# Attention's entry of a hybrid S5 and attention layer: keys in turn with the first queries, values last, y's copies issued later

## The chip, the cores and the metric

The kernel runs on one core of a Trainium2 chip. The metric is the device time of one execution in microseconds (us). The kernel before was timed three times: 1645.6, 1643.4 and 1640.19 us, median 1643.4 us.

## The reference

The layer takes two sequences of 512 tokens (one "prompt", one "sample", treated alike) with model width 1024 and computes, in float32:

```python
h = rms_norm(x, ln1)
q, k, v, u, g_att, g_ssm = jnp.split(h @ w_in, IN_SPLITS, axis=-1)
q = rms_norm(q.reshape(bsz, seq_len, N_HEADS, HEAD_DIM), q_gain)       # 16 heads of 64
k = rms_norm(k.reshape(bsz, seq_len, N_KV_HEADS, HEAD_DIM), k_gain)    # 4 key-value heads
y_att = windowed_attention(q, k, v, sink, bias, mask)   # blocks of 128 queries, 3 blocks of keys
y_ssm = s5_branch(u, ...)                               # scan both ways, gelu, then GLU with w_glu
mixed = sigmoid(g_att) * y_att + sigmoid(g_ssm) * y_ssm
x = x + mixed @ w_out
h2 = rms_norm(x, ln2)
return x + square(relu(h2 @ w_up)) @ w_down
```

The windowed attention adds a relative bias to the scores, takes a softmax with a sink logit for each head and multiplies with the values. A query head's norm runs over its own 64 columns.

## The kernel before

All 1024 tokens are handled together. A float32 product is made from three matmuls of rounded parts: every operand is split into a high part (a copy that rounds it, ACT) and a low part (the rest, a subtraction on DVE), and high x high, high x low and low x high are summed in PSUM. So each weight that is loaded costs, besides its DMA into a raw tile (`w_raw`, or `c_raw` for a 128-column block; both in the tag `c_raw`, two buffers), a cast on ACT and a subtraction on DVE.

The program runs in this order: the norm, the gates and u; the S5 branch, whose result y goes to DRAM (`y_scr`); attention, with the S5 branch's GLU entering at its end; w_out; the MLP. The change is at the seam between the S5 branch and attention, lines 499 to 762.

**Attention's entry before.** The keys' weights are loaded (`load_qkv`, L519) into the pool `cpool`, tags `c_hi` and `c_lo`, two halves of 4 x 128 rows each; then eight key tiles K0 to K7 of 128 tokens are projected (`proj_qkv`, 24 matmuls of 128x256 each, lines 164 to 166) into a PSUM slot `acc` (three of them) and normed (`head_rms`, L503: square on ACT, sum on DVE L509, add and power on POOL L511 and L512, product on DVE L514 into `kn`). The values follow in the same manner, with weights in the pool `ap`, tiles V0 to V7, copied out by ACT (L551) and DVE (L552). Then come the eight copies that reorder y in DRAM (`y2_scr` from `y_scr`, L744 and L745, 512 KB each, issued from SP), the query weights of the first key-value head (`weight_pieces(0)`, four pieces of 256 rows, into `cpool`), four bias tables (L582), and the turned keys (`key_copies` on POOL L588, `key_turn`: four transposes on PE L597, a copy on ACT L598, a subtraction on DVE L599).

Last in the entry, four query tiles Q0 to Q3 of the first step are made one after the other (L752 to L762). A tile (class `Tile`) is projected (24 matmuls, L615), squared (ACT L621), summed (DVE L625), raised to a power (POOL L627, L628), multiplied (DVE L632), doubled by a copy (POOL L633) and turned (four transposes on PE into a slot `acc`, L638), then copied out by ACT (L643) and DVE (L647). For Q0 to Q2 the turn stands right behind the tile's own norm; Q3's turn is left for the first step.

**The steps.** There are eight steps, one for each key-value head and sequence, and four units of 128 queries in each. PE, ACT and DVE follow an order written out by hand (L778 on): a unit's scores (L668), maximum (DVE L672), exponentials (ACT L678), while PE also turns the previous unit's weights and multiplies with its values and projects a query tile of the next step between them. SP and POOL follow an order that the scheduler chooses. One piece of a later step's query weights is loaded in each unit (`pieces_of`); in all of this `weight_pieces(j)` uses `cpool` for even heads j and `ap` for odd ones. In the second unit of a step the previous step's sums are inverted and sent through DRAM (`rs_scr` L729, `fac` L734), and POOL multiplies the step's output by them (L739, 128x1024 elements) and SP writes it (`mix_scr`, L740).

**The end of attention.** The reordered y is loaded in eight pieces (`yr`, L889) and cast (ACT L894, DVE L895), and the GLU begins (L901 on): its weight columns go through `cpool`'s `c_hi` and `c_lo` (L137 to L139), and its inputs `mx` are loaded from DRAM (L909).

## Time and profile before

| | us |
|---|---|
| median of three runs | 1643.4 |
| the profiled execution, its own time | 1645.35 |
| its span (first to last instruction) | 1643.5 |
| PE busy in the span | 1524.7 |
| DVE busy | 1145.3 |
| ACT busy | 796.1 |
| POOL busy | 172.8 |

The profiled execution's mean granted TensorE clock is 0.975 of full speed. In a row of the timeline the first two numbers are the start and the duration in us, counted from the start of the span; the bracket gives the idle time of the engine just before and what ended it. In the list of waits, the three numbers are the total, the count and the longest. In a table of windows, each engine has its busy time and, in brackets, its number of instructions, and PEclk is the share of full speed that the clock gate granted.

In the trace, the first key tile of the entry's uninterrupted part (K3) starts at 479.69 us, the keys' turn follows the last value tile at 518.51 us, the first query tile starts at 520.39 us, and the second unit of the first step starts its scores at 560.10 us.

### The profile page before, as it was taken

Reading aid. Unit: us, or ns where it says so; the run is one execution under the profiler, and the core shown is the slowest. Engines: PE = TensorE matmul, PEld = TensorE weight load, DVE = VectorE, ACT = ScalarE, POOL = GpSimd, SP = SyncE. Lnnn points to the kernel's source line nnn. Section 1 sums busy time; section 2 is a strip of 40 time slices with the busy share of each in tenths; the row PEclk is TensorE's granted clock in tenths of the full one; section 3 lists DMA queues with packets and bytes.
Section 4 is the critical chain, followed back from the end, with each engine's and each line's share of the span. In section 5 each row is a group of like instructions: output and inputs, shape, how many; then the busy total and the mean of one; then the engine's idle time right before and its main releaser. Section 6 shows DMA issues by size and latency. Waiting matters only on the chain.

```text
span 1643.5 us, 22428 instructions
## 1 busy us (share of the span) xinstructions
PE 1524.7 (93%) x8202; PEld 1295.5 (79%) x8202; DVE 1145.3 (70%) x2006; ACT 796.1 (48%) x1398; POOL 172.8 (11%) x246
## 2 busy tenths in 40 slices
PE   4999999999778799998788998999999999999999
PEld 3778878888777798896565898788888888888787
DVE  7899969952432488989787564877777759666644
ACT  5667752222322488878555322555445544433332
POOL 2000001000021233332354000000000000000000
PEclk9999999999889899999889999999999999999999
DMA  4444457224772021223556322355444397445331
GB/s 156 130 149 150 143 176 270 90 103 133 270 248 88 14 71 46 92 66 103 199 192 221 132 91 103 116 159 162 160 142 146 118 353 273 154 133 187 118 126 64
DMA packets 115226, 240.24 MB, mean 146 GB/s; under 512 B 15355, under 2 KB 38011, under 8 KB 115116
## 3 DMA queue, kind: packets, MB, share of 16 engines
q1 hardware_dynamic: 93100, 191.47, 36.3%
q10 hardware_dynamic: 19456, 37.87, 6.1%
q0 software_dynamic: 2560, 9.48, 1.7%
q8 instruction: 64, 1.05, 0.2%
q14 instruction: 46, 0.38, 0.1%
HBM read 169.53 MB, written 81.82 MB: 153 GB/s over the span
## 4 chain that ended last, share of the span: by engine, by line
PE 72%; DVE 9%; DMA 6%; issue 6%; ACT 4%; POOL 2%; SPq 0%; ACTq 0%; POOLq 0%; DVEq 0%
PE bank L165 12%; PE bank L164 12%; PE bank L166 12%; PE acc L164 7%; PE acc L165 7%; PE acc L166 7%; PE acc L615 4%; DMA ctab_in<-ct_scr 2%; PE sps L389 2%; PE sps L409 2%; PE po L700 2%; PE sps L487 2%; PE sps L668 1%; PE tps L684 1%; PE acc L638 1%
## 5 line engine op out<-in xcount | busy, mean ns | idle before, releaser
L165 PE MATMUL bank<-b_lo,a_hi 128*128 128x512 f32 x448 | 174.7, 390 | 1.4 <-DVE b_lo L1118 1.4
L166 PE MATMUL bank<-b_hi,a_lo 128*128 128x512 f32 x448 | 174.3, 389 | 0.0
L164 PE MATMUL bank<-b_hi,a_hi 128*128 128x512 f32 x448 | 173.5, 389 | 0.0
L165 PE MATMUL acc<-hT,c_hi 128*128 128x512 f32 x384 | 152.1, 396 | 0.0
L164 PE MATMUL acc<-hT,c_hi 128*128 128x512 f32 x384 | 151.9, 396 | 0.0
L166 PE MATMUL acc<-hT,c_lo 128*128 128x512 f32 x384 | 150.2, 391 | 0.4 <-DVE c_lo L139 0.4
L164 PE MATMUL bank<-act,u_hi 128*128 128x512 f32 x376 | 147.2, 392 | 2.6 <-ACT u_hi L1015 2.6
L165 PE MATMUL bank<-act,u_hi 128*128 128x512 f32 x376 | 146.9, 391 | 0.0
L1117 ACT CAST a_hi<-d_a 128x1024 fp32r<-128x1024 f32 x56 | 59.2, 1057 | 181.1 <-PE bank L165 177.9
L166 PE MATMUL bank<-act,u_lo 128*128 128x512 f32 x376 | 146.6, 390 | 0.0
L1118 DVE TENSOR_TENSOR a_lo<-d_a,a_hi 128x1024 fp32r<-128x1024 f32 x56 | 68.5, 1224 | 99.2 <-ACT a_hi L1117 99.2
L615 PE MATMUL acc<-w_hi,hT 128*128 128x256 f32 x512 | 121.2, 305 | 3.6 <-ACT w_hi L573 3.6
L165 PEld LDWEIGHTS bank<-b_lo,a_hi 128*128 128x128 f32 x448 | 84.1, 188 | 19.9 <-DVE b_lo L1118 2.6
L164 PEld LDWEIGHTS bank<-b_hi,a_hi 128*128 128x128 f32 x448 | 84.1, 188 | 17.6
L166 PEld LDWEIGHTS bank<-b_hi,a_lo 128*128 128x128 f32 x448 | 84.1, 188 | 17.4
L615 PEld LDWEIGHTS acc<-w_hi,hT 128*128 128x128 f32 x512 | 91.1, 199 | 7.8 <-ACT w_hi L573 4.0
L139 DVE TENSOR_TENSOR c_lo<-c_raw,c_hi 128x512 fp32r<-128x512 f32 x80 | 62.5, 785 | 46.0 <-ACT c_hi L138 45.7
L138 ACT CAST c_hi<-c_raw 128x512 fp32r<-128x512 f32 x80 | 49.2, 620 | 81.0 <-PE acc L165 56.1
L164 PEld LDWEIGHTS bank<-act,u_hi 128*128 128x128 f32 x376 | 71.0, 189 | 18.0 <-ACT u_hi L1015 3.2
L164 PEld LDWEIGHTS acc<-hT,c_hi 128*128 128x128 f32 x384 | 72.3, 188 | 15.6 <-issue 1.5
L166 PEld LDWEIGHTS acc<-hT,c_lo 128*128 128x128 f32 x384 | 72.1, 188 | 15.3 <-DVE c_lo L139 0.7
L165 PEld LDWEIGHTS acc<-hT,c_hi 128*128 128x128 f32 x384 | 72.3, 188 | 15.1 <-issue 1.1
(292 smaller groups left out, 3909.5 us busy)
## 6 DMA issues: line engine op xcount, KB each, us to landing
d_a<-a_scr SPq DMA_DIRECT2D x56, 512.0 KB
u_raw<-in_w_up_dram SPq DMA_DIRECT2D x32, 512.0 KB
a_scr<-t ACTq DMA_DIRECT2D x64, 256.0 KB
k<-in_w_down_dram SPq DMA_DIRECT2D x32, 512.0 KB
c_raw<-in_w_ug_dram SPq DMA_DIRECT2D x48, 256.0 KB
a_scr<-a ACTq DMA_DIRECT2D x48, 256.0 KB
ct_scr<-ctab SPq DMA_DIRECT2D x16, 576.0 KB
ctab_in<-ct_scr SPq DMA_DIRECT2D x16, 576.0 KB
```

The costliest lines, as they stand in the source:

```text
L138: S.copy(hi[:, sl, :], raw)
L139: sub(lo[:, sl, :], raw, hi[:, sl, :].bitcast(F32))
L164: PE.matmul(ps, a[0], b[0], start=first, stop=False)
L165: PE.matmul(ps, a[0], b[1], start=False, stop=False)
L166: PE.matmul(ps, a[1], b[0], start=False, stop=last)
L389: PE.matmul(ps[0:48, g * 144:(g + 1) * 144], lbt[:, ri, q * SG + gp * SH + g, :], ctab[:, gp * SH + g, ri].rearrange("p n c -> p (n c)"), ...
L409: PE.matmul(ps[:, i * P:(i + 1) * P], bm[:, ri, g, :], u_sb[:, gp * SH + g, :], start=True, stop=True)
L487: PE.matmul(o, ctab[:, g0 % SI + g, ri, 0:T * CH], st[:, ri, g].rearrange("p s k -> p (s k)"), start=False, stop=ri == 1)
L615: PE.matmul(self.ps, hT[sq][act][:, k, col:col + P], w[:, k % 4, :], start=i == 0, stop=i == 3 * KT - 1)
L700: PE.matmul(self.po, vv, self.hl[i][part], start=i + part == 0, stop=i == self.nkb - 1 and part == 1)
L1117: S.copy(hi, src)
L1118: V.tensor_sub(lo, src, hi.bitcast(F32))
```

## The change

The entry is written in another order. The four key tiles of the first sequence come first; then each query tile Q0 to Q3 is followed by one of the key tiles K4 to K7, and a query tile is turned only after the next query tile's projection. The keys are turned after K4. The values' weights and V0 to V7 come last. The values' weights now go half into the two buffers of the tag `ev` and half into `cpool`; the query weights of even heads go into `ap` and of odd heads into `cpool`, the other way round than before. y's eight copies are written one to a unit in the second and third steps (i = 1 and 2).

```diff
-        def load_qkv(src, even):
+        def load_qkv(src, homes):
             halves = []
             for e in range(2):
-                pool = cpool if even else ap
-                hi = pool.tile([P, KT // 2, CB], F32R, tag="c_hi", name="w_hi")
-                lo = pool.tile([P, KT // 2, CB], F32R, tag="c_lo", name="w_lo")
+                pool, tags = homes[e]
+                hi, lo = [pool.tile([P, KT // 2, CB], F32R, tag=tag, name=name) for tag, name in zip(tags, ("w_hi", "w_lo"))]
...
-        def rows_blocks(blk, fn):
-            w = load_qkv(w_qkv[blk], blk == K_BLK)
-            for t in range(NT):
-                ps = acc()
-                proj_qkv(ps[:, 0:CB], w, hT[t // 4], (t % 4) * P)
-                fn(t, ps[:, 0:CB])
-
-        rows_blocks(K_BLK, lambda t, ps: head_rms(ps, kn[:, t]))
+        def rows_block(w, t, fn):
+            ps = acc()
+            proj_qkv(ps[:, 0:CB], w, hT[t // 4], (t % 4) * P)
+            fn(t, ps[:, 0:CB])
+
+        def k_evac(t, ps):
+            head_rms(ps, kn[:, t])
...
-        rows_blocks(V_BLK, v_evac)
...
-            pool = cpool if j % 2 == 0 else ap
+            pool = ap if j % 2 == 0 else cpool
...
-        for t in range(T):
-            SP.dma_start(y2_scr[:, :, t, :].rearrange("g c k -> c g k"), y_scr[t])
-
+        column = cpool, ("c_hi", "c_lo")
+        w_k = load_qkv(w_qkv[K_BLK], [column, column])
+        for t in range(4):
+            rows_block(w_k, t, k_evac)
         for piece in weight_pieces(0):
             piece()()
         load_biases(0)
-        key_turn(0, 0, key_copies(0, 0))
+        kd = key_copies(0, 0)
         rows = None
         for t in range(4):
             new = Tile(0, 0, t)
             new.project(3 * KT)
             new.square()
             new.power()
             new.norm()
-            if t < 3:
-                new.turn()
-                new.high()
-                new.low()
-        rows = new
+            if rows:
+                rows.turn()
+                rows.high()
+                rows.low()
+            rows = new
+            rows_block(w_k, 4 + t, k_evac)
+            if t == 0:
+                key_turn(0, 0, kd)
+        w_v = load_qkv(w_qkv[V_BLK], [(evp, ("ev", "ev")), column])
+        for t in range(NT):
+            rows_block(w_v, t, v_evac)
...
                 for qb in range(NB):
+                    if 1 <= i < 3:
+
+                        t = (i - 1) * NB + qb
+                        SP.dma_start(y2_scr[:, :, t, :].rearrange("g c k -> c g k"), y_scr[t])
```

Three places show what this makes of the engines' order. The first is PE at the turn of query tile Q0. Before, the transposes (L638) stand between the last matmuls of Q0 (`acc_4649`) and the first of Q1 (`acc_4691`):

```order
L615 MATMUL acc_4649<-w_lo_4620,hT0_0_109 128x256
L615 MATMUL acc_4649<-w_hi_4619,hT0_1_110 128x256
L638 MATMUL acc_4684<-ident_89,qn_4681 128x128 x4
L615 MATMUL acc_4691<-w_hi_4609,hT0_0_109 128x256
L615 MATMUL acc_4691<-w_lo_4610,hT0_0_109 128x256
```

In the changed kernel the same transposes (now L634, `qn_4295` is Q0's) stand behind all of K4, the turn of the keys and all of Q1 (`acc_4341`), and K5 (`acc_4383`, lines 164 to 166) follows:

```order
L611 MATMUL acc_4341<-w_lo_4244,hT0_0_109 128x256
L611 MATMUL acc_4341<-w_hi_4243,hT0_1_110 128x256
L634 MATMUL acc_4376<-ident_89,qn_4295 128x128 x4
L164 MATMUL acc_4383<-w_hi_4081,hT1_0_111 128x256
L165 MATMUL acc_4383<-w_lo_4082,hT1_0_111 128x256
L166 MATMUL acc_4383<-w_hi_4081,hT1_1_112 128x256
```

PE's whole sequence was K3 to K7, V0 to V7, the keys' turn, Q0, its turn, Q1, two scores of the first unit, Q1's turn, Q2, its turn, Q3; it is now K3, Q0, K4, the keys' turn, Q1, Q0's turn, K5, Q2, Q1's turn, K6, Q3, Q2's turn, K7, V0 to V7, and then the first unit.

The second place is SP, which issues the loads, around the first step's division (`row` into `rs_scr`, then `fac`, then `mix_scr`). Before, with all of y's copies issued long ago:

```order
L572 DMA w_raw<-in_w_qkv_dram 128x512 x7
L729 DMA rs_scr<-row 16x128
L734 DMA fac<-rs_scr 64x2x512 x2
L572 DMA w_raw<-in_w_qkv_dram 128x512
L740 DMA mix_scr<-ya 128x2x512
L582 DMA bias<-line_scr 128x384 x4
```

In the changed kernel (y's copies are L791, and a row prints both y buffers as `y_scr`):

```order
L791 DMA y_scr<-y_scr 16x64x128
L725 DMA rs_scr<-row 16x128
L568 DMA w_raw<-in_w_qkv_dram 128x512 x2
L791 DMA y_scr<-y_scr 16x64x128
L730 DMA fac<-rs_scr 64x2x512 x2
L578 DMA bias<-line_scr 128x384 x4
L736 DMA mix_scr<-ya 128x2x512
```

The load of `fac` now stands behind two loads of query weights and the last copy of y. The copies do not stand one to a unit as they are written: the scheduler has put the first ahead of the values' weights, the second and third between and behind these, and the others between the loads of the first and second steps' query weights.

The third place is POOL, at the same division's product. Before, it stands in the third unit of the second step, ahead of a tile's sum (`ms_5526`), and the turned keys' copy `kd_5674` of the third step comes eight instructions later:

```order
L660 COPY p_5635<-nsink_103 128x4
L739 TENSOR_TENSOR ya_4813<-ya_4813,fac_5389 128x1024
L627 TENSOR_SCALAR ms_5526<-ms_5526 128x4
L628 TENSOR_TENSOR rq_5528<-ms_5526,neg_half_94 128x4
L633 COPY qn_5558<-qn_5558 128x4x64
L660 COPY p_5744<-nsink_103 128x4
L627 TENSOR_SCALAR ms_5639<-ms_5639 128x4
L628 TENSOR_TENSOR rq_5641<-ms_5639,neg_half_94 128x4
L660 COPY p_5852<-nsink_103 128x4
L588 COPY kd_5674<-kn_4079 128x512
L633 COPY qn_5671<-qn_5671 128x4x64
```

In the changed kernel it stands right ahead of that copy, in the first unit of the third step:

```order
L656 COPY p_5742<-nsink_103 128x4
L623 TENSOR_SCALAR ms_5636<-ms_5636 128x4
L624 TENSOR_TENSOR rq_5638<-ms_5636,neg_half_94 128x4
L656 COPY p_5851<-nsink_103 128x4
L735 TENSOR_TENSOR ya_4805<-ya_4805,fac_5383 128x1024
L584 COPY kd_5671<-kn_4079 128x512
L629 COPY qn_5668<-qn_5668 128x4x64
```

From the next division on, POOL's order is that of before. One more thing moves far from the entry: since `cpool` now holds the odd heads' query weights, the casts of the GLU's first two weight columns (L138 on ACT, L139 on DVE, four of each) leave the fifth and sixth steps, where they stood among the units; they now stand in the last unit of the seventh step, in the eighth step, and, for the second column's subtractions, behind nearly all of the casts of `yr`.

## The prediction

> **What bounds the kernel now.** I read the page's totals first, and in the chain of work that ended last the shares by engine:

> ```profile
> PE 1524.7 (93%) x8202; PEld 1295.5 (79%) x8202; DVE 1145.3 (70%) x2006; ACT 796.1 (48%) x1398; POOL 172.8 (11%) x246
> PE 72%; DVE 9%; DMA 6%; issue 6%; ACT 4%; POOL 2%; SPq 0%; ACTq 0%; POOLq 0%; DVEq 0%
> ```

> PE bounds the whole, so the question is where PE stands still or runs slowly near the change. Next come the waits between 470 and 590 us, the rows with PE as the waiting engine:

> ```profile
> PE acc L638 <- POOL qn L633: 11.3, 5, 3.3
> ...
> PE acc L164 <- DVE kn L514: 4.2, 1, 4.2
> ...
> PE acc L615 <- ACT w_hi L573: 3.6, 2, 2.3
> ...
> PE acc L615 <- DVE w_lo L574: 1.0, 3, 0.5
> ```

> The 4.2 us is the wait ahead of K3, which stands at the same place in both orders. The other three rows are the four query tiles: 4.6 us for their weights, and 11.3 us for the normed tile ahead of each turn. Then the table of windows: the keys and values, the first query tile, the rest of the query tiles with the first unit, the second unit up to the next step, the steps after that, and the last step with the GLU's start.

> ```profile
> core 0: us, PE busy (x) PEld busy (x) DVE busy (x) ACT busy (x) POOL busy (x), PEclk, DMA share, GB/s
> 479.70:518.90 39.20, 39.20 (x316) 39.17 (x316) 10.44 (x24) 6.14 (x16) 10.39 (x15) 0.96 0.54 155
> 518.90:528.40 9.50, 4.86 (x26) 3.66 (x24) 3.76 (x6) 3.14 (x6) 0.00 (x0) 0.93 0.34 109
> 528.40:557.70 29.30, 18.21 (x105) 17.49 (x104) 7.34 (x19) 6.60 (x14) 7.17 (x13) 0.73 0.02 8
> 557.70:588.60 30.90, 30.36 (x225) 28.16 (x226) 26.40 (x66) 24.65 (x61) 7.91 (x17) 1.00 0.10 32
> 588.60:740.00 151.40, 147.89 (x1090) 136.25 (x1089) 133.74 (x348) 122.30 (x306) 53.48 (x94) 1.00 0.23 72
> 740.00:814.80 74.80, 63.98 (x325) 50.61 (x324) 58.77 (x120) 56.44 (x112) 20.10 (x23) 0.93 0.43 139
> ```

> In the third row PE is busy for 18.21 of 29.30 us, and at a clock of 0.73. So the query tiles lose twice: by waiting, and by running slowly after it. The timeline of PE shows how:

> ```profile
> 531.80 1.12 PE L638 MATMUL acc<-ident,qn 128*128 128x128 f32 x4 [3.28 <-POOL qn L633]
> ...
> 534.42 0.63 PE L615 MATMUL acc<-w_hi,hT 128*128 128x256 f32 x2
> 534.85 0.41 PE L615 MATMUL acc<-w_lo,hT 128*128 128x256 f32 x1
> ...
> 541.32 1.12 PE L638 MATMUL acc<-ident,qn 128*128 128x128 f32 x4 [3.11 <-POOL qn L633]
> ...
> 545.43 0.40 PE L615 MATMUL acc<-w_hi,hT 128*128 128x256 f32 x2
> 545.67 0.28 PE L615 MATMUL acc<-w_lo,hT 128*128 128x256 f32 x1
> 545.79 0.28 PE L615 MATMUL acc<-w_hi,hT 128*128 128x256 f32 x1
> 549.41 0.66 PE L638 MATMUL acc<-ident,qn 128*128 128x128 f32 x4 [3.35 <-POOL qn L633]
> ...
> 557.74 0.66 PE L638 MATMUL acc<-ident,qn 128*128 128x128 f32 x4 [1.39 <-POOL qn L633]
> 558.23 0.60 PE L597 MATMUL tps<-ident,kd 128*128 128x128 f32 x4
> 558.59 0.36 PE L615 MATMUL acc<-w_hi,hT 128*128 128x256 f32 x1
> ...
> 560.10 0.34 PE L668 MATMUL sps<-kh,qa 128*128 128x384 f32 x1
> ```

> Two matmuls take 0.43 us (534.42 to 534.85) after the first idle stretch, and 0.24 us (545.43 to 545.67) at full speed. The four waits for `qn` are 3.28 + 3.11 + 3.35 + 1.39 = 11.13 us; the 11.3 has one short wait more. With 4.6 us for the weights, PE waits 15.7 us in the entry.

> **The change part by part.** (1) **The entry.** I count PE's work from K3's start at 479.7 us to the second unit's scores at 560.1 us, 80.4 us. It is 5 key, 8 value and 4 query tiles and one tile of the next step: 18 x 24 = 432 matmuls of 0.12 us, 51.8 us; six turns of 0.36 us (558.23 to 558.59), 2.2 us; eight matmuls of scores, 1.0 us. Together 55.0 us. The rest, 80.4 - 55.0 = 25.4 us, is 15.7 us of waits and 9.7 us of half clock. Of the half clock some stays: the stretch up to 518.9 us has 13 tiles, 312 x 0.12 = 37.4 us, and the keys' turn, yet lasts 39.2 us. Its surplus, 39.2 - 37.4 - 0.4 = 1.4 us, follows the unchanged wait ahead of K3. So 25.4 - 1.4 = 24.0 us can go.

> Does it go? The turn of a query tile needs this chain, here for the third tile, whose last matmul starts at 545.79:

> ```profile
> 546.16 0.39 ACT L621 ACTIVATE sq<-acc 128x256 f32<-128x256 f32 x1 [3.00 <-PE acc L615]
> ...
> 547.40 1.04 POOL L628 TENSOR_TENSOR rq<-ms,neg_half 128x4 f32<-128x4 f32 x1
> 548.47 0.42 DVE L632 TENSOR_TENSOR qn<-acc,rq 128x256 f32<-128x256 f32 x1 [1.47 <-POOL rq L628]
> 548.96 0.40 POOL L633 COPY qn<-qn 128x256 f32<-128x256 f32 x1 [0.52 <-DVE qn L632]
> ```

> The turn starts 3.62 us after that matmul. Now two tiles stand between, 2 x 24 x 0.12 = 5.8 us: covered with 2 us to spare. The tighter chain is that of the three slots `acc`. A tile's slot is free when DVE's product ends, 548.89, some 3.0 us after PE could go on (545.91); in the new order one tile and one turn stand between the end of a slot's use and the next, 2.88 + 0.36 = 3.24 us. That leaves 0.2 us, and DVE also does the values' and queries' low parts there (about 0.7 us each, in its idle time mostly). Likewise the second half of the values' weights can be cast only after K7 has read its own, and PE has 30 matmuls of V0 to V2 (3.6 us) to do meanwhile. If all is hidden this costs nothing; if each of the eight slots in the alternation came 0.3 us late, 2.4 us. I take 0.6, near the hidden end, since the margin is positive. The query weights' 4.6 us goes: their loads stand ahead of y's copies in SP's order now. Before, they stood behind all of them:

> ```profile
> 481.02 11.44 SPq L745 DMA_DIRECT2D y_scr<-y_scr  x7
> 494.44 2.60 SPq L572 DMA_DIRECT2D w_raw<-in_w_qkv_dram  x2
> ```

> [...]

> (2) **The first unit's exponentials.** Before, they ran between the stalled query tiles:

> ```profile
> 537.69 0.28 PE L668 MATMUL sps<-kl,qa 128*128 128x256 f32 x1
> ...
> 538.58 1.28 ACT L678 ACT_TABLE_LOAD   x1 [0.43 <-DVE nmx L672]
> 539.88 0.51 ACT L678 ACTIVATE p<-p,nmx 128x257 f32<-128x257 f32 x1
> ...
> 558.87 0.69 ACT L598 ACTIVATE kh<-tps,gain_k 128x512 fp32r<-128x512 f32 x1 [2.31 <-PE tps L597]
> ```

> That cover is gone. ACT's table load starts 0.9 us after the scores, when the first maximum is there (538.58 - 537.69). Then ACT needs 1.28 us for it, 4 x 0.6 for the exponentials with their sums, and for the turned keys and Q3, which stand between them, 2 x 0.69: 6.0 us after the first scores. Meanwhile PE has 8 x 0.12 + 24 x 0.12 + 2 x 0.36 = 4.6 us of the first unit and 0.7 us of the second's scores (560.10 on, four of 128x384) before it turns the weights. So 0.7 us late, and a little more by the backlog on ACT and DVE: I take 1.0, between 0 and 2.

> (3) **POOL.** The division's product moves ahead of the third step's `kd` and `qn`:

> ```profile
> 602.52 2.41 POOL L739 TENSOR_TENSOR ya<-ya,fac 128x1024 f32<-128x1024 f32 x1 [0.40 <-DMA fac<-rs_scr]
> ...
> 614.05 0.61 POOL L588 COPY kd<-kn 128x512 f32<-128x512 f32 x1
> 614.61 0.40 POOL L633 COPY qn<-qn 128x256 f32<-128x256 f32 x1
> ```

> PE turns that tile at 615.06, when the copy of 614.61 has just ended, so it will stand 2.4 us; behind it wait the turn of the keys and all of PE's order. PE is busy 147.89 of 151.40 us there, so nothing gives it back. `fac` itself is issued later, behind two loads of weights and a copy of y, but has some 10 us until POOL gets there. I take 2.3, between 0 and 2.4.

> (4) **The GLU's first two columns.** Four casts (ACT) and four subtractions (DVE) leave a stretch where PE is nearly full and come into the last 75 us, where PE has 64 us of work, ACT 56 and DVE 59, and the chain goes back and forth. One of each:

> ```profile
> 695.42 0.62 ACT L138 CAST c_hi<-c_raw 128x512 fp32r<-128x512 f32 x1
> 807.00 0.69 DVE L139 TENSOR_TENSOR c_lo<-c_raw,c_hi 128x512 fp32r<-128x512 f32 x1 [2.01 <-ACT c_hi L138]
> ```

> 4 x 0.69 = 2.8 us is the most if DVE is the one that waits there; nothing if they fit its gaps. The third column's loads come later by their two buffers, too, about 1 us. I take 1.5, between 0 and 3.8.

> (5) **y's copies and the weights' homes** cost nothing by themselves: the copies are asynchronous, the DMA's share in the steps they move to is 0.02 to 0.23, and y is not read before the last steps.

> **The sum:** 24.0 - 0.6 - 1.0 - 2.3 - 1.5 = 18.6 us. The profiled execution (1645.35 us, of which 1643.5 is the span) would go to 1626.8; it stands 2 us above the median of the runs, so the median goes from 1643.4 to 1624.8, say 1625.

> **The rivals.** (a) All the covers hold: the product on POOL and the GLU's casts are hidden, and only part (2) costs. Gain 22 to 24 us, 1619 to 1621. For it speaks that the engines beside PE have idle time; against it that PE's turn at 615.06 had no slack at all.

> (b) The alternation doesn't run free: the slots `acc` come late by up to a microsecond at each of the eight tiles between K3 and V0, since ACT, DVE and POOL each take key and query tiles in strict order. Another 4 to 8 us, 1629 to 1633.

> (c) The clock doesn't come back. PE would wait a little at every tile, too short to matter by itself, but often. The matmuls from K3's end to the second unit, about 52 us, would take 52/0.73 = 71 us at the clock of the third row of windows: 19 us lost, 1644, no change. From a clock of about 0.64 on (81 us, 29 lost) it ends slower, and at 0.5 it is 1625 + 52 = 1677. Against it: in the steps after 588.6, PE has many short waits (3.5 of 151 us) at a clock of 1.00. [...]

> (d) The copies of y aren't spread as the change says: three of eight stand on SP among the entry's weights, and one each before the division's transfers. If these hold up the values' weights by a copy's share of the 11.44 us (1.6 us) each, that is 2 to 5 us more, 1627 to 1630.

> **How the numbers follow.** The forecast, with its own range of 1621 to 1628, has 0.58; (a) 0.14; (b) 0.11 and (d) 0.09; (c) 0.04 for no change and 0.04 for slower. About 0.3% (5 us) is what a measurement of this kernel can tell from no change. So faster is 0.92, same 0.04, slower 0.04. The range takes in (a) with the scatter of the runs below, and (b) above: 1617 to 1633.

> **What would show it.** In the changed profile: no wait of PE above 0.5 us between K3 and V7; a clock of 1.00 from about 483 us on; the second unit's scores at about 537 us instead of 560; a wait of PE for POOL's `kd` or `qn` of about 2.3 us some 55 us after that; and PE's wait at the GLU's start about as long as now. Waits for `kn` or `qn` at every tile would mean (b), a clock under 0.9 there (c), a wait for the values' weights (d).

## The result, and the profile after

The changed kernel takes 1624.5 us (median of four runs, 1619.4 to 1630.8) where the kernel before takes 1644.5 us in the same comparison (four runs). The ratio is 0.988 with an interval of 0.983 to 0.992. A second comparison on another occasion gave 1619.9 against 1643.0 us, ratio 0.985 (0.982 to 0.988). The prediction was 1625 us, faster.

The page of the changed kernel begins with the same picture as before, PE in front:

```profile
PE 1522.8 (93%) x8202; PEld 1293.8 (79%) x8202; DVE 1140.7 (70%) x2006; ACT 794.0 (49%) x1398; POOL 172.7 (11%) x246
```

Busy times hardly move (PE 1522.8 us after 1524.7): a PE that waits isn't counted as busy, so a wait that goes doesn't show in them. The span is only 14.5 us shorter than in the profile before, so it must be cut into pieces first. I cut at three events of PE: the start of K3, the first scores of the first step's second unit, and PE's restart after its long wait in the GLU. Here are those rows of the changed kernel's timeline, with the turns between them:

```profile
484.34 0.58 PE L164 MATMUL acc<-w_hi,hT 128*128 128x256 f32 x1 [4.18 <-DVE kn L514]
495.30 0.60 PE L593 MATMUL tps<-ident,kd 128*128 128x128 f32 x4
498.60 0.60 PE L634 MATMUL acc<-ident,qn 128*128 128x128 f32 x4
504.79 0.60 PE L634 MATMUL acc<-ident,qn 128*128 128x128 f32 x4
511.30 0.60 PE L634 MATMUL acc<-ident,qn 128*128 128x128 f32 x4
...
542.74 0.34 PE L664 MATMUL sps<-kh,qa 128*128 128x384 f32 x1
...
811.47 0.79 PE L164 MATMUL acc<-act,c_hi 128*128 128x512 f32 x1 [11.47 <-ACT c_hi L138]
```

No turn has a bracket any more: PE waits for no query tile in the entry. Before, K3 started at 479.69, the second unit at 560.10 and the GLU's restart was at 827.08. So the pieces are:

| us | before | after | difference |
|---|---|---|---|
| start to K3 | 479.7 | 484.3 | +4.7 |
| stage 1: K3 to the second unit's scores | 80.4 | 58.4 | -22.0 |
| stage 2: from there to the GLU's restart | 267.0 | 268.7 | +1.8 |
| the rest | 816.4 | 817.5 | +1.1 |
| span | 1643.5 | 1629.0 | -14.5 |

The first piece and the last wander: over all profiles shown below K3 starts between 475.0 and 484.3 us, whichever kernel it is, and the rest takes 814 to 821 us. Stage 1 and stage 2 are what the change touches. The waits of PE between 470 and 570 us are down to two rows:

```profile
PE acc L164 <- DVE kn L514: 4.2, 1, 4.2
...
PE sps L664 <- DVE nmx L668: 0.5, 1, 0.5
```

The first is the unchanged wait ahead of K3. The windows of the changed kernel, cut at the corresponding places (columns as before), show the clock:

```profile
484.30:523.50 39.20, 39.07 (x303) 38.60 (x304) 17.39 (x35) 10.62 (x22) 18.05 (x28) 0.93 0.35 101
523.50:536.00 12.50, 12.50 (x107) 12.50 (x106) 1.94 (x5) 1.86 (x5) 0.00 (x0) 1.00 0.29 88
```

PE is full from K3 on, and slow only at the start (0.93): the clock of 0.73 that stood over the query tiles is gone. The one new wait in the steps is that for POOL's product, in the timelines of POOL and PE:

```profile
596.97 2.37 POOL L735 TENSOR_TENSOR ya<-ya,fac 128x1024 f32<-128x1024 f32 x1
599.29 0.60 POOL L584 COPY kd<-kn 128x512 f32<-128x512 f32 x1
599.84 0.40 POOL L629 COPY qn<-qn 128x256 f32<-128x256 f32 x1
...
600.29 0.66 PE L634 MATMUL acc<-ident,qn 128*128 128x128 f32 x4 [2.19 <-POOL qn L629]
```

The product has no bracket: it waits for no load of `fac` and stands late by POOL's order alone. It ends, the two copies follow at once, and PE's turn starts when the second is done, after 2.19 us of standing still.

### The profile page after: what moved, and what is told of

It reads as the page before. It is cut to its first block, busy times and chain, and to the rows that moved or that the text cites. A ratio compares the mean times of both kernels' runs of the same rounds, so it can differ in the third digit from the quotient of the medians.

```text
span 1629.0 us, 22424 instructions
## 1 busy us (share of the span) xinstructions
PE 1522.8 (93%) x8202; PEld 1293.8 (79%) x8202; DVE 1140.7 (70%) x2006; ACT 794.0 (49%) x1398; POOL 172.7 (11%) x246
## 4 chain that ended last, share of the span: by engine, by line
PE 72%; DVE 8%; DMA 7%; issue 6%; ACT 4%; POOL 2%; SPq 0%; ACTq 0%; POOLq 0%; DVEq 0%
PE bank L165 12%; PE bank L166 12%; PE bank L164 12%; PE acc L165 7%; PE acc L166 7%; PE acc L164 7%; PE acc L611 4%; DMA ctab_in<-ct_scr 3%; PE sps L389 2%; PE sps L409 2%; PE sps L487 2%; PE po L696 1%; DMA k<-in_w_down_dram 1%; PE sps L664 1%; PE tps L680 1%
## 5 line engine op out<-in xcount | busy, mean ns | idle before, releaser
L164 PE MATMUL bank<-b_hi,a_hi 128*128 128x512 f32 x448 | 174.2, 391 | 0.0
L164 PE MATMUL acc<-hT,c_hi 128*128 128x512 f32 x384 | 152.6, 397 | 0.0
L164 PE MATMUL bank<-act,u_hi 128*128 128x512 f32 x376 | 147.6, 393 | 3.3 <-ACT u_hi L1022 3.3
L611 PE MATMUL acc<-w_hi,hT 128*128 128x256 f32 x512 | 116.1, 295 | 0.0
L164 PEld LDWEIGHTS bank<-b_hi,a_hi 128*128 128x128 f32 x448 | 84.5, 189 | 17.5
L139 DVE TENSOR_TENSOR c_lo<-c_raw,c_hi 128x512 fp32r<-128x512 f32 x80 | 60.9, 765 | 43.1 <-ACT c_hi L138 42.9
L611 PEld LDWEIGHTS acc<-w_hi,hT 128*128 128x128 f32 x512 | 87.0, 189 | 3.8
L138 ACT CAST c_hi<-c_raw 128x512 fp32r<-128x512 f32 x80 | 49.1, 618 | 83.5 <-PE acc L165 47.5
L164 PEld LDWEIGHTS bank<-act,u_hi 128*128 128x128 f32 x376 | 71.2, 189 | 18.7 <-ACT u_hi L1022 3.7
L164 PEld LDWEIGHTS acc<-hT,c_hi 128*128 128x128 f32 x384 | 72.7, 189 | 15.6 <-issue 1.5
```

What stands on the lines that cost most here:

```text
L138: S.copy(hi[:, sl, :], raw)
L139: sub(lo[:, sl, :], raw, hi[:, sl, :].bitcast(F32))
L164: PE.matmul(ps, a[0], b[0], start=first, stop=False)
L611: PE.matmul(self.ps, hT[sq][act][:, k, col:col + P], w[:, k % 4, :], start=i == 0, stop=i == 3 * KT - 1)
```

## The experiments

**The changed kernel once more.** No edit; it shows how far stages can be trusted.

> The changed kernel once more, to see how far the stages of two profiles agree. Stage 1 is the time from K3's first matmul to the first scores of the first step's second unit, stage 2 from there to PE's restart after its long wait in the GLU (11 to 12 us). In the two profiles so far stage 1 is 80.4 us before and 58.4 after, stage 2 is 267.0 before and 268.7 after. All theories: 58.4 +- 1 and 268.7 +- 1, whatever comes ahead of K3 (which started 4.7 us later in the profile after). If the stages themselves wander by several us, the sum of the prediction met the median by chance.

Measured: stage 1 58.35 us, stage 2 270.98 us. K3 started at 477.21 us, 7 us earlier than in the first profile, and stage 1 is the same to 0.1 us. Stage 2 is 2.3 us longer than in the first profile, more than expected: 2.0 us of it are in its last part, from the turn of the keys in the seventh step on (96.5 against 94.5 us). So stage 1 is the sharper instrument, though two profiles of the kernel before, below, differ by 1.6 us in it; stage 2 can be trusted only as far as the seventh step.

**y's copies behind the values.** The changed kernel with:

```diff
         w_v = load_qkv(w_qkv[V_BLK], [(evp, ("ev", "ev")), column])
         for t in range(NT):
             rows_block(w_v, t, v_evac)
+        for t in range(T):
+            SP.dma_start(y2_scr[:, :, t, :].rearrange("g c k -> c g k"), y_scr[t])
...
-                    if 1 <= i < 3:
-
-                        t = (i - 1) * NB + qb
-                        SP.dma_start(y2_scr[:, :, t, :].rearrange("g c k -> c g k"), y_scr[t])
```

> The changed kernel with y's eight copies written behind the values' tiles instead of in the second and third steps. POOL's product for the first division then stands where it stood before, and the load of fac directly behind rs_scr. Theory: PE's wait of 2.19 us for the third step's qn goes, stage 2 falls from 268.7 to 266.5, stage 1 stays at 58.4 and the whole is some 2 us faster than the changed kernel. Rival (the spread of y's copies itself brings part of the gain): stage 1 rises by 2 us or more, since six copies in a row stand ahead of the next query weights, and the whole is no faster.

Measured: 1618.3 us, ratio to the kernel before 0.984 (0.981 to 0.987); the changed kernel in the same comparison 1619.9 (0.985). Stage 1 57.5, stage 2 265.3. In its timeline POOL's product is back in the second step and PE's turn in the third step doesn't wait:

```profile
581.72 2.40 POOL L735 TENSOR_TENSOR ya<-ya,fac 128x1024 f32<-128x1024 f32 x1 [0.62 <-DMA fac<-rs_scr]
...
593.59 0.40 POOL L629 COPY qn<-qn 128x256 f32<-128x256 f32 x1
...
594.04 0.66 PE L634 MATMUL acc<-ident,qn 128*128 128x128 f32 x4
```

The time between the turns of the keys in the second and third steps is 28.9 us, as in the kernel before, against 31.2 in both profiles of the changed kernel. So the spread of the copies costs 2.3 us there and brings nothing to stage 1, which is even 0.9 us shorter without it: here the half clock lasts 3.0 us from K3's start on, in the changed kernel 5.1. The whole, 1.7 us less, goes the same way, but the intervals overlap, and the whole alone would not show it.

**The spread of y's copies alone.** The kernel before, with the eight copies taken out of the entry and the four lines of the change put into the steps.

> The kernel before with one part of the change alone: y's copies written in the second and third steps. The query weights are then loaded long before the query tiles. Theory: the 4.6 us of waits for the weights go, with the little half clock that follows them (0.5 us), and the waits for qn and their half clock stay: stage 1 falls from 80.4 to about 75.3. POOL's product moves just as in the changed kernel, so stage 2 rises by 2.2. The whole gains about 3 us. Rival (the copies are what the entry suffers from): stage 1 falls by 10 us or more.

Measured: 1638.6 us, ratio 0.9975 (0.9959 to 0.9991). Stage 1 71.7 us, which lies between the two theories. The waits for the weights are gone and those for `qn` are not:

```profile
523.10 0.66 PE L638 MATMUL acc<-ident,qn 128*128 128x128 f32 x4 [3.28 <-POOL qn L633]
530.22 0.66 PE L638 MATMUL acc<-ident,qn 128*128 128x128 f32 x4 [3.11 <-POOL qn L633]
538.60 1.12 PE L638 MATMUL acc<-ident,qn 128*128 128x128 f32 x4 [3.34 <-POOL qn L633]
...
606.98 1.11 PE L638 MATMUL acc<-ident,qn 128*128 128x128 f32 x4 [2.18 <-POOL qn L633]
```

The first three waits are those of before to 0.02 us (a fourth of 1.37 us follows), but four transposes take 0.66 us at the first two turns and 1.12 at the third. The clock fell to half twice, at 531.64 us, behind the second turn, and at 538.46, ahead of the third, each time for 3.4 us; behind the first wait, of 3.28 us, it didn't fall at all. The window of these tiles has a clock of 0.88, not 0.73:

```profile
520.00:549.20 29.20, 18.27 (x124) 17.64 (x125) 7.82 (x20) 7.63 (x17) 7.17 (x13) 0.88 0.00 1
```

So of the 8.7 us gained in stage 1, 4.6 are waits, as expected, and most of the other 4 lie in the clock, which is at half for 9.7 us of stage 1 here and for 20.0 before (PE waits through part of these). The last row above is PE's turn in the third step. It waits 2.2 us here as well, with nothing of the entry's order changed: POOL's new place comes with the copies. The transposes behind that wait take 1.11 us, because the clock fell there too (606.73 to 610.14 us). Stage 2 is 271.9 us, 4.9 above that of before, where I had expected 2.2.

**Turns one query tile later, alone.** The kernel before with:

```diff
-            if t < 3:
-                new.turn()
-                new.high()
-                new.low()
-        rows = new
+            if rows:
+                rows.turn()
+                rows.high()
+                rows.low()
+            rows = new
```

> The kernel before, with each query tile's turn written behind the next query tile's projection, and nothing else: no key tiles between. One tile of 2.9 us covers the chain of 3.6 us that cost 3.1 to 3.4 us each time. Theory: three waits of 0.5 to 1 us and the fourth of 1.4 are left, waits that short leave the clock at full, and the 4.6 us for the weights stay: stage 1 falls from 80.4 to 66 or 67. Rival (only other tiles between the query tiles, or the copies of y, bring the gain): stage 1 stays above 75.

Measured: 1629.9 us, ratio 0.992 (0.989 to 0.994). Stage 1 65.0 us. The rows of PE's waits from 478 to 545 us:

```profile
PE acc L615 <- ACT w_hi L573: 2.9, 2, 1.7
PE acc L638 <- POOL qn L633: 2.1, 1, 2.1
PE sps L668 <- DVE nmx L672: 1.3, 1, 1.3
PE acc L615 <- DVE w_lo L574: 0.4, 1, 0.4
```

Stage 1 is 1 us under what I expected. One wait for `qn` is left instead of four, though a longer one (2.1 us) than the 0.5 to 1 us that I had for each: PE's order had the first two query tiles interleaved, so that Q1 covered less of Q0's chain. From 482.2 us on, behind K3's slow start, the clock is 1.00. This one edit brings 15.4 of the 22 us of stage 1.

**The kernel before, once more.**

> The kernel before, profiled once more. With y's copies alone moved, the waits for qn were the same as before (11.1 us), but the clock fell to half only after the third one, not after the first two: 0.88 in that stretch, not 0.73. Theory (the half clock after a wait of 3.1 to 3.4 us depends on where the wait falls): the waits are again 4.6 and 11.1 us, but the share of half clock may be anything from 3 to 10 us, so stage 1 lies between 73.5 and 81. Rival (the order of the loads decides the clock): stage 1 is 80.4 within 1 us.

Measured: stage 1 82.0 us. The waits are 11.1 us for `qn` and 4.9 for the weights, and at each of the first three turns the clock is at half (four transposes take 1.12, 1.11 and 1.11 us):

```profile
524.00:553.00 29.00, 19.25 (x103) 18.49 (x102) 6.38 (x15) 5.97 (x12) 5.29 (x11) 0.67 0.04 12
```

That is 1 us above the range that I gave, and outside the rival's as well. The clock is at half for 23.5 us of stage 1, against 20.0 in the first profile, and half of these 3.5 us makes up the difference of 1.6. So for one and the same order the variation that is shown is 1.6 us. The larger one, of 3 to 4 us, is shown only between two orders with the same waits for `qn`. The last section shows ahead of which stretches at half clock PE stood still, and for how long; whether the order or chance puts the waits where they do so stays open.

**Matmuls in the waits.** The kernel before, with this ahead of `new.turn()`:

```diff
             if t < 3:
+                warm = ps_o.tile([P, 512], F32, tag="po", name="warm")
+                for n in range(22):
+                    PE.matmul(warm[:, 0:CB], hT[0][0][:, 0, t * P:(t + 1) * P], weights[0][0][0][:, 0, :], start=True, stop=True)
                 new.turn()
```

> The kernel before, with 22 matmuls of 128x256 added behind each of Q0, Q1 and Q2, whose result nothing reads (they go into the PSUM slot of the attention's output, which is free there). They fill most of PE's waits for the weights and for qn. Theory (waits and half clock are two separate losses): the waits stay, as filled time, and the half clock goes: stage 1 is 71 to 74, the clock 1.00 between the query tiles. Rival (the slow matmuls are not due to PE's standing still): stage 1 is 80 or more.

Measured: 1640.0 us, ratio 0.998 (0.997 to 0.999). Stage 1 75.5 us, 1.5 above the theory's range and well under the rival's. Its windows over the wait for the weights and over the query tiles:

```profile
518.50:527.00 8.50, 6.96 (x40) 6.26 (x40) 3.17 (x6) 3.32 (x6) 0.00 (x0) 0.80 0.28 85
527.00:551.50 24.50, 21.06 (x166) 19.70 (x164) 6.71 (x16) 5.40 (x11) 6.37 (x12) 1.00 0.08 22
```

Between the query tiles the clock is 1.00, with the same chain ahead of every turn; of each wait for `qn` some 1.1 us is left unfilled. The clock still fell where the weights are waited for (1.28 and 0.26 us, then half speed from 522.06 on), and there the added matmuls themselves ran slowly (seven take 1.60 us at 524.12 us, sixteen 2.39 us at 528.34). So in this entry the slow matmuls between the query tiles come from PE's standing still, and they are a loss of their own, beside the waits.

**Turns one place earlier.** The changed kernel with each turn behind the key tile that follows its query tile:

```diff
-            if rows:
-                rows.turn()
-                rows.high()
-                rows.low()
-            rows = new
             rows_block(w_k, 4 + t, k_evac)
             if t == 0:
                 key_turn(0, 0, kd)
+            if t < 3:
+                new.turn()
+                new.high()
+                new.low()
+        rows = new
```

> The changed kernel with each query tile's turn one place earlier: behind the key tile that follows it, not behind the next query tile as well. A tile of 2.9 us then covers the chain of 3.6 us. Theory: PE waits 0.6 to 0.8 us ahead of each of three turns (the first has the keys' turn as 0.4 us more of cover), the clock stays at 1.00, stage 1 rises from 58.4 to 60 or 60.5. Rival (short waits between groups of matmuls bring the half clock back): the clock falls under 0.9 and stage 1 is above 64.

Measured: stage 1 60.2 us, with this row among PE's waits from 474 to 562 us:

```profile
PE acc L634 <- POOL qn L629: 1.4, 3, 0.8
```

The window over the alternation has a clock of 1.00:

```profile
488.00:516.00 28.00, 26.76 (x219) 25.87 (x218) 12.50 (x24) 7.96 (x17) 12.02 (x19) 1.00 0.22 64
```

As the theory had it, one tile is not quite enough to cover the chain, and three waits of at most 0.8 us left the clock at 1.00. The waits are 1.4 us in all, though, where 1.8 to 2.4 were expected.

**Matmuls in the wait ahead of K3.** The version with y's copies behind the values, and 16 matmuls, ready when the query weights' first cast is:

```diff
-        for t in range(4):
+        for t in range(3):
             rows_block(w_k, t, k_evac)
-        for piece in weight_pieces(0):
+        pieces = weight_pieces(0)
+        for piece in pieces[:2]:
+            piece()()
+        warm = ps_o.tile([P, 512], F32, tag="po", name="warm")
+        for n in range(16):
+            PE.matmul(warm[:, 0:CB], hT[0][0][:, 0, n % 4 * P:(n % 4 + 1) * P], weights[0][0][0][:, 0, :], start=True, stop=True)
+        rows_block(w_k, 3, k_evac)
+        for piece in pieces[2:]:
             piece()()
```

> The version with y's copies behind the values, with 16 matmuls added in PE's wait of 4.2 us ahead of K3, whose result nothing reads. They start when the query weights' first cast is done, about in the middle of the wait. Theory: K3 then runs at full speed; of the 1.3 to 2.1 us of half clock that follow the wait, about 1 us is gained, since Q0 will then wait for the second half of its weights a little: stage 1 falls from 57.5 to 56.5 (58.4 is the other value seen, with a longer stretch at half clock). Rival: the clock falls all the same, because half of the wait is still idle, and stage 1 is 57.5 to 58.5.

Measured: 1618.9 us, ratio 0.986 (0.984 to 0.987). K3 starts at 474.95 and the second unit at 533.37: stage 1 58.4 us, 0.9 more than without the matmuls. The clock did come back; it is 1.00 up to the second unit. The first rows of the windows from the added matmuls on, and then PE's waits:

```profile
470.70:474.90 4.20, 2.23 (x17) 1.96 (x16) 1.54 (x4) 2.08 (x5) 1.83 (x3) 1.00 0.41 155
474.90:480.00 5.10, 4.69 (x37) 4.49 (x37) 2.37 (x6) 1.30 (x3) 2.92 (x4) 1.00 0.64 178
480.00:486.00 6.00, 5.63 (x47) 5.63 (x48) 2.67 (x7) 2.06 (x5) 3.23 (x6) 1.00 0.69 193
```

```profile
PE acc L611 <- DVE w_lo L570: 0.7, 1, 0.7
PE acc L164 <- DVE kn L514: 0.7, 2, 0.5
PE acc L165 <- DVE w_lo L530: 0.7, 1, 0.7
...
PE acc L634 <- POOL qn L629: 0.2, 1, 0.2
```

Neither theory had this: the slow stretch is gone, and PE waits 2.1 us in new small pieces, mostly for DVE's parts of the weights and for a slot that `kn` holds (the rows without 0.25 us of the second row, which lies ahead of K3). DVE gets no faster: it starts Q0's product 10.48 us after K3 (485.43), and 10.51 us in the version without the matmuls (491.84). So in the changed kernel the alternation has no slack. The slow start of K3 had given DVE and POOL the time that they need.

## Why the prediction was right

The stages by kernel, from the timelines of PE. The medians come from three comparisons, in which the kernel before had 1644.5, 1643.0 and 1642.4 us. "Third step" is the time from the turn of the keys in the second step to that in the third; "tail" is from the turn of the keys in the seventh step to the GLU's restart.

| kernel | median of the whole | stage 1 | third step | tail |
|---|---|---|---|---|
| before | 1644.5 | 80.4 | 28.9 | 95.2 |
| before, second profile | 1641.8 (one run) | 82.0 | 28.9 | 94.9 |
| changed | 1624.5 | 58.4 | 31.2 | 94.5 |
| changed, second profile | 1619.9 | 58.4 | 31.2 | 96.5 |
| y's copies behind the values | 1618.3 | 57.5 | 28.9 | 94.0 |
| spread of the copies alone | 1638.6 | 71.7 | 32.1 | 95.8 |
| later turns alone | 1629.9 | 65.0 | 28.9 | 95.7 |
| matmuls in the waits | 1640.0 | 75.5 | 28.9 | 100.5 |
| earlier turns | 1630.3 (one run) | 60.2 | 31.4 | 94.3 |
| matmuls ahead of K3 | 1618.9 | 58.4 | 28.9 | 94.2 |

The forecast had a gain of 18.6 us; the medians give 20.0, and 23.0 on the second occasion, whose 1619.9 us lie a little under the forecast's own range of 1621 to 1628 and within the whole one of 1617 to 1633.

**The entry** was right in its cause, and in its size by errors that cancelled. The sum left 58.0 us for stage 1 (80.4 - 24.0 + 0.6 + 1.0), and 58.4 was measured twice. Both losses are real. That the half clock would go with the waits, as the 24.0 us have it, no run had shown when the sum was made. With later turns alone most of the waits for `qn` went (11.1 us before, 2.1 left) and the clock is 1.00 from 482.2 us on; with matmuls in the waits the clock alone came back, to 1.00 from 527.0 to 551.5 us. Within the sum the terms were off and met. The window of all of stage 1 in the changed kernel:

```profile
484.34:542.74 58.40, 58.31 (x465) 57.84 (x465) 21.86 (x50) 16.54 (x37) 18.05 (x28) 0.96 0.30 87
```

PE stands idle for 0.1 us, where the slots (0.6) and the exponentials (1.0) had been given 1.6. The half clock that stays was put at 1.4 us; it lasted from K3's start to 489.4 us, 5.1 us at half speed, so 2.5 were lost. The rest, 55.8 us, is PE's work, 0.8 more than I had counted. So 1.5 us too much and 1.9 too little leave the 0.4 by which the sum was short. For the exponentials these rows show that nothing was lost on PE:

```profile
539.04 1.28 ACT L674 ACT_TABLE_LOAD   x1 [0.44 <-DVE nmx L668]
...
542.98 0.49 ACT L674 ACTIVATE p<-p,nmx 128x257 f32<-128x257 f32 x1
...
543.43 0.60 PE L680 MATMUL tps<-ident,p 128*128 128x128 f32 x4
```

The first unit's scores begin at 538.03. The last exponential ends 5.4 us later (542.98 + 0.49), not 6.0, and PE comes to turn the weights 5.4 us later too, not 5.3: the chain was some 0.6 us shorter than I had put it together, and only just hidden.

**The slots.** The 0.6 us for late slots were not lost; that the margin is positive but small was right, and the last experiment shows how small. The margin would have been used up if K3 had run at full speed.

**POOL** was right: 2.3 us predicted, 2.2 waited, 2.3 in the step's length. The cause is shown: the product goes back when y's copies leave the steps, and it moves when the copies alone are moved. What the sum left out is the clock behind this wait. In both profiles of the changed kernel it stayed up (the four transposes behind waits of 2.19 and 2.18 us take 0.66 us); in the run with the copies alone and in the one with earlier turns, with waits of 2.18 and 2.21 us, it fell to half for 3.4 us, and the third and fourth steps together took some 1.7 us more (62.8 and 62.9 us against 61.0 and 61.2).

**The GLU's columns** were mis-sized. I took 1.5 us; the tail is 94.0 to 96.5 us with the casts late and 94.9 to 95.8 with them early (100.5 once, in the kernel with the added matmuls, for a cause that stays open). No cost can be seen. Nothing takes these casts alone, so this rests on the comparison of tails only.

**The copies of y** were said to cost nothing by themselves. That was wrong by the 2.3 us that the sum had under POOL: both are one thing. Rival (d) expected that they hold up the values' weights; no wait for these is in the changed profile. Rival (a) was nearly right about the entry, but PE did stand for POOL; (b) and (c) didn't happen, and (c)'s premise, that waits of under a microsecond bring the clock down, has the run with earlier turns against it (three waits of at most 0.8 us, clock 1.00).

## What to carry to other kernels

A tile whose result needs a chain over three engines wants other tiles on PE until the chain is done: count the chain from the last matmul to the first one that needs it, and the work between; one tile of 2.9 us against 3.6 us was not enough, two were. A transfer that is moved carries along what the scheduler orders by it: look at every queue behind it, not at its bytes. And before filling an idle stretch to keep the clock up, ask whether the engines behind it could follow a faster PE. In the kernel that was filled here they could not: PE waited 2.1 us in new places.

## What was not expected of the hardware

```profile
517.98:521.39 3.41, 1.84 (x16) 1.64 (x14) 0.91 (x2) 0.38 (x1) 0.53 (x2) 1.00 0.03 7
521.39:524.81 3.42, 1.71 (x15) 1.71 (x16) 0.72 (x2) 0.69 (x1) 1.14 (x2) 1.00 0.00 0
528.22:531.64 3.42, 1.42 (x12) 1.42 (x13) 0.43 (x2) 2.33 (x6) 1.35 (x2) 1.00 0.00 0
531.64:535.05 3.41, 3.41 (x18) 3.38 (x16) 0.76 (x1) 0.00 (x0) 0.00 (x0) 0.50 0.00 0
603.32:606.73 3.41, 1.48 (x11) 1.11 (x9) 2.20 (x7) 1.58 (x5) 3.21 (x4) 1.00 0.00 0
606.73:610.14 3.41, 3.16 (x14) 3.06 (x15) 0.43 (x1) 1.15 (x2) 0.20 (x1) 0.50 0.42 156
```

The first two pieces share the first wait for `qn`, of 3.28 us; PE is busy for 1.84 and 1.71 us of them, and the clock stays. The third piece has most of the second wait, PE is busy for 1.42 us, and the next piece is at half. The fifth has nearly all of the wait of 2.18 us for POOL, PE is busy for 1.48 us, and half clock follows; in the changed kernel the same wait falls on two pieces, with PE busy for 2.89 and 1.75 us, and the clock stays. Between 470 and 615 us of all ten profiles, every piece at full clock with PE busy for 1.5 us or less is followed by one at half, and of those with 1.6 us or more a single one (1.87 us, in the kernel with matmuls in its waits). Elsewhere in the changed kernel half speed follows a piece with 1.87 us (from 755.64 us on) and full speed one with 1.63 us (from 837.57 us on), so no exact threshold is shown.

So in these profiles the length of a wait does not decide alone. To read from the timeline of before that half speed follows its waits of 3.11 to 4.2 us, and not that of 1.39, would be too simple: there the clock falls at 527.0 us, ahead of the first wait for `qn`, among the waits for the weights (2.32, 0.34 and 0.21 us). The wait of 4.2 us ahead of K3, longer than a piece, was followed by half speed in every profile but the one that filled it, and for a varying time: 13 matmuls before, 23 in the changed kernel. So a part of what such a change gains hangs on where the waits happen to fall; I estimate it at 3 to 4 us here, from the 8.7 us of stage 1 that the copies alone brought, of which 4.6 are waits.
